# Tiles of the block products, and the planned spacing of the S5 input blocks

## Chip, core and metric

The kernel runs on one core of a Trainium2 chip. The metric is the device time of one execution in microseconds (us), and the figure quoted is the median over runs. The engines are TensorE (PE, with its weight loads as PEld), VectorE (DVE), ScalarE (ACT) and GpSimd (POOL); SyncE (SP) issues nearly all DMAs.

## What is computed

One layer of an encoder block on a sequence of 1024 positions with 1024 features, float32:

```python
xn = rmsnorm(h)
u, z_a, v, b_g, c_g, z_b, g_a, g_b = split(xn @ w_in)        # w_in is 1024 x 8192
y = D*u + S5_forward(u) + S5_backward(u)                      # 64 groups of 16 features, 64 states
y = gelu(y); y = y * sigmoid(y @ w_glu); y_a = y * silu(z_a)
y_b = b_g * (conv3(c_g * v) + conv_b) * silu(z_b)
merged = sigmoid(g_a) * (y_a @ w_branch_a) + sigmoid(g_b) * (y_b @ w_branch_b)
out = rmsnorm(h + merged @ w_out)
```

## The kernel before, in words

Each float32 matrix is split into a high and a low part, and a product is three products of parts (high x high, high x low, low x high), each over eight blocks of 128. One matmul here is 128 x 128 by 128 x 512.

The work goes by stages. First the input is normalised and turned, and the tables of the S5 branch are built. Then come the **projections**: 36 items of 48 matmuls each, one for every 128 columns of most of `w_in`. An item loads 512 KB of weights (`wr_p`), and most items store 512 KB of results to DRAM. Beside the items runs the **S5 branch**, in 16 blocks of four groups. An input block (`input_block`, line 534) loads two tables of 512 KB, `bdt_x` and `pwt_x`, and 256 KB of `u`; DVE joins the tables (lines 554 to 557), PE multiplies (`xps`, line 566) and ACT puts the result into the states. After four input blocks DVE runs the scan; then for each block come the output map, the correction `ks` (lines 578 and 580, behind the matmuls `kf` and `kb`) and the output products `yps` (line 594). `bdt_x` and `pwt_x` have two buffers each, so a `bdt` load waits for PE's use of the block before the last, and a `pwt` load for DVE's work on it.

The order of PE's and DVE's instructions is the order in which the code issues them. It is set by estimates: `est["pe"]` and `est["dve"]` count planned microseconds, and `at["t"]` (line 574) says when the next input block is due. Work of an engine that is not so fixed (ACT, SP) is placed by the scheduler.

Behind the projections the rest of `w_in` is done as **block products** (`gates`, `seven`). A pair of column blocks takes seven products of 12 matmuls (a Strassen form) instead of eight: in order `B11`, `T2`, `T1`, `T3`, `B21`, `B22`, `T4`. Each goes to a PSUM tile; DVE adds it into the results (`plus`). There are 12 pairs in `pairs7`. Some products read combined inputs `sx0` to `sx3` that DVE and ACT build beforehand (`combinations`, lines 833 to 841 and 806, 807): `sx2` and `sx3` only once all S5 work is out. The weights of a pair are combined one pair ahead by `prep`; those of the first pair are made during the last item. While a pair runs, DVE also does the convolution and the gating of earlier pairs (`jobs`); so pairs are fuller or lighter for DVE, by turns of three.

PSUM holds eight banks of 512 columns: four single tiles (`bank`, turned round in order) and two wide tiles of two banks each (`mm_tile`). In a pair, `T1` and `T3` are the two halves of one wide tile and `T4` is half of the other; the other four products are in single banks.

After the pairs come four products of the whole size: with `w_branch_b` (its input `yb` is read back from DRAM), with `w_glu`, with `w_branch_a`, and with `w_out`, and then the last normalisation.

Of the kernel before, what the change touches and what calls it, by code (L numbers as in the profile page):

```python
# [45 lines left out]
def bcast(ap, axis, n):  # L46
    shape = list(ap.shape)
    shape.insert(axis, n)
    return ap.unsqueeze(axis).to_broadcast(shape)
# [3 lines left out]
def block_kernel(  # L53
# [32 lines left out]
    def bank(name):  # L86
        return bgp.tile([P, 512], F32, tag="bg", name=name)

    def mm_tile(name):
        return mmp.tile([P, D], F32, tag="mm", name=name)  # L90
# [80 lines left out]
    with ExitStack() as st:  # L171
# [150 lines left out]
        f = math.factorial  # L322
# [176 lines left out]
    est = {"pe": 0.0, "dve": 6.0}  # L499
    parts = []  # L500

    def vec(us):
        est["dve"] = max(est["dve"], est["pe"]) + us

    def part(ready, us, fn):
        p_ = {"ready": ready, "us": us, "fn": fn, "end": None}
        parts.append(p_)
        return p_
# [11 lines left out]
    def ssm(sp, other):  # L520
# [3 lines left out]
        def load_u(blk, name):  # L524
            U = sp.tile([P, 4, P], F32, tag="U", name=f"U_{name}", bufs=3)
            base = ud[blk // 2][:, :]
            nc.sync.dma_start(out=U, in_=bass.AP(tensor=base.tensor, offset=base.offset + 4 * (blk % 2) * H * D,
                                                 ap=[[P, P], [H * D, 4], [1, P]]))
            return U

        SBs, lasts = {}, {}
        at = {"n": 0, "t": 20.0}

        def input_block():
            n = at["n"]
            q = n // 4
            if n % 4 == 0:
                SBs[q] = turn_p.tile([P, P, 2, GQ], F32, tag=f"Y{q % 2}", name=f"SB{q}")
            SB = SBs[q]
            nm = f"x{n}"  # L540
            U = load_u(n, nm)
            rep = []
            for src, outer, tag in ((bd, [[NG * 2 * P, H], [0, T]], "X0"), (pw, [[0, H], [NG * 2 * P, T]], "X2")):
                r_ = turn_p.tile([P, 4, 2, P], F32, tag=f"X{int(tag[1]) + n % 2}", name=f"{'bdt' if src is bd else 'pwt'}_{nm}")
                base = src[:, :]
                nc.sync.dma_start(
                    out=r_, in_=bass.AP(tensor=base.tensor, offset=base.offset + 4 * n * 2 * P,
                                        ap=outer + [[1, 4 * 2 * P]]))
                rep.append(r_)

            g_ = sp.tile([P, 4, 2, P], F32, tag="dv", name=f"g_{nm}", bufs=1)
            Wi, pw_ = rep
            er, ei = (bcast(pw_[:, :, ri], 2, 2) for ri in range(2))
            V.tensor_tensor(out=g_, in0=Wi, in1=er, op=ALU.mult)
            V.tensor_tensor(out=pw_, in0=Wi[:, :, ::-1], in1=ei, op=ALU.mult)
            V.tensor_tensor(out=Wi[:, :, 0], in0=g_[:, :, 0], in1=pw_[:, :, 0], op=ALU.subtract)
            V.tensor_tensor(out=Wi[:, :, 1], in0=g_[:, :, 1], in1=pw_[:, :, 1], op=ALU.add)
            vec(3.8)
            gl = 4 * (n % 4)

            def into():
                for ri in range(2):
                    xps = bank(f"xps{ri}_{nm}")
                    x3 = xps.rearrange("p (j c) -> p j c", j=4)
                    for j in range(4):
                        nc.tensor.matmul(out=xps[:, P * j:P * j + P], lhsT=Wi[:, j, ri, :],  # L566
                                         rhs=U[:, j, :], start=True, stop=True)
                    dst = SB[:, :, ri, gl:gl + 4].rearrange("p k g -> p g k")
                    S.copy(out=dst[0:NG], in_=x3[0:NG])  # L569
                    S.copy(out=dst[NG:P, :, ::-1], in_=x3[NG:P])  # L570

            lasts[q] = part(est["dve"] + 0.5, 1.8, into)
            at["n"] += 1
            at["t"] = max(at["t"], est["pe"] - 6.0) + 8.0

        def lags(b):
            ks, kf, kb = b["ks"], b["kf"], b["kb"]
# [239 lines left out]
    HK = K // 2  # L817
    half = (slice(0, 512), slice(512, D))
# [94 lines left out]
    def seven(p, w):  # L913

        sx = late["S"]
        u, i = pairs7[p]
        A = lambda o, h: [(xnh[o + k][:, half[h]], xnl[o + k][:, half[h]]) for k in range(HK)]
        o_ = [held(q, f"v{i + q}") if u == 2 else t4(f"go{p}_{q}") for q in range(2)]
        at = lambda q, h: o_[q][:, half[h]]
        wide = {}  # L920

        def prod(n, xs, place=None):
            if place is None:
                ps = bank(f"g{n}_{p}")
            else:
                if place[0] not in wide:
                    wide[place[0]] = mm_tile(f"gw{place[0]}_{p}")
                ps = wide[place[0]][:, half[place[1]]]
            for k in range(HK):
                for i_, (l, r) in enumerate(((0, 0), (0, 1), (1, 0))):  # L930
                    nc.tensor.matmul(out=ps, lhsT=w[n][l][:, k, :], rhs=xs[k][r],  # L931
                                     start=k == 0 and i_ == 0, stop=k == HK - 1 and i_ == 2)
            est["pe"] += 12 * 0.2266
            return ps

        def plus(q, h, ps, in_, end=False):
            V.tensor_tensor(out=at(q, h), in0=ps, in1=in_, op=ALU.add)  # L937
            vec(0.66)
            if end and u >= 6:
                S.activation(out=at(q, h), in_=at(q, h), func=AF.Sigmoid)  # L940

        g = prod("B11", A(0, 0))
        yield 0
        S.copy(out=at(0, 0), in_=g)
        g = prod("T2", sx["2"])
        yield 1
        plus(0, 1, g, at(0, 0))
        g = prod("T1", sx["1"], (0, 0))
        yield 2
        plus(1, 0, g, at(0, 1))  # L950
        g = prod("T3", sx["3"], (0, 1))
        yield 3
        plus(1, 1, g, at(1, 0), True)
        plus(0, 1, g, at(0, 1))
        g = prod("B21", A(HK, 0))
        yield 4
        plus(0, 0, g, at(0, 0), True)
        g = prod("B22", sx["4"])
        yield 5
        plus(1, 0, g, at(1, 0), True)  # L960
        g = prod("T4", A(HK, 1), (1, 0))
        yield 6
        plus(0, 1, g, at(0, 1), True)
        if u >= 6:
            for q in range(2):
                nc.sync.dma_start(out=(gbd if u == 7 else gad)[i + q], in_=o_[q])
        elif u == 2:
            vs[:] = o_
        elif u == 4:
            later_c(i, o_, vs)  # L970
        elif u == 3:
            later_b(i, o_)
# [115 lines left out]
    for i in range(K):  # L1088
        ps = product(w_branch_b[0][:, P * i:P * i + P], ybh, ybl, f"ob{i}")
# [25 lines left out]
    for i in range(K):  # L1115
        ps = product(w_glu[0][:, P * i:P * i + P], ygh, ygl, f"glu{i}", ks=ks)
# [21 lines left out]
    for i in range(K):  # L1138
        ps = product(w_branch_a[0][:, P * i:P * i + P], yah, yal, f"oa{i}")
# [30 lines left out]
    for h in range(2):  # L1170
        for t in range(T):
# [3 lines left out]
            for c, (o, n) in enumerate(cuts):  # L1175
                ps = bank(f"o{h}_{t}_{c}")
# [57 lines left out]
```

## Time and profile before

| | |
|---|---|
| Time, three runs | 1186.35 us median (1179.81 to 1187.08) |
| The profiled execution | 1184.2 us, span 1182.4 us |
| PE busy | 1132.7 us, 96% of the span |
| DVE busy | 818.7 us, 69% |
| ACT busy | 462.4 us, 39% |
| DMA | 167.79 MB, 138 GB/s of HBM over the span |

Matmuls overlap, so PE's busy time says only that it seldom stands still; how fast it goes is read from the starts of successive rows in its timeline. A wait is shown in square brackets behind the row that it delays, with what ended it.

### The profile page before, as it was taken

The numbers are of one execution on the slowest core, as the hardware profiler recorded it, in microseconds if no ns is written. First come the engines' busy times: TensorE is split into PE (matmuls) and PEld (weight loads), VectorE is DVE, ScalarE is ACT, GpSimd is POOL, SyncE is SP. The second block draws the span as 40 slices with busy tenths as digits, with TensorE's granted clock in tenths as the row PEclk, the third lists the DMA queues.
The fourth block names the chain that finished last, engine by engine and source line by source line (L and its number), as shares of the span: only waits on it lengthen the run. The fifth ranks groups of instructions, "written<-read, shape, count | busy, mean of one in ns | idle before, by whom it ended". The sixth has DMA issues, their size and how long they took to land.

```text
span 1182.4 us, 15042 instructions
## 1 busy us (share of the span) xinstructions
PE 1132.7 (96%) x5782; PEld 935.1 (79%) x5782; DVE 818.7 (69%) x1303; ACT 462.4 (39%) x556; POOL 14.4 (1%) x59
## 2 busy tenths in 40 slices
PE   6999989999999999999899999999999999999997
PEld 4777868888888888888677777777788888887886
DVE  6856579768877997877786868777378347446234
ACT  6343761664276255174332222223255225123111
POOL 2000000000000000000000000000000000000000
PEclk9999999999999999999899999999999999999999
DMA  8339983377347335433423141416757434227002
GB/s 265 95 134 259 253 232 116 125 207 190 116 132 195 116 104 152 124 99 107 143 60 118 43 135 36 142 36 230 268 184 252 169 107 139 93 89 261 6 36 106
DMA packets 166459, 167.79 MB, mean 142 GB/s; under 512 B 11852, under 2 KB 138996, under 8 KB 166260
## 3 DMA queue, kind: packets, MB, share of 16 engines
q1 hardware_dynamic: 166244, 166.65, 46.0%
q8 instruction: 45, 0.74, 0.2%
q14 instruction: 26, 0.21, 0.1%
q10 hardware_dynamic: 144, 0.20, 0.0%
HBM read 119.63 MB, written 42.99 MB: 138 GB/s over the span
## 4 chain that ended last, share of the span: by engine, by line
PE 85%; DVE 6%; DMA 4%; issue 2%; ACT 2%; SPq 0%; POOL 0%; POOLq 0%; DVEq 0%; ACTq 0%
PE ps_p L136 30%; PE gB L931 8%; PE ps_glu L136 7%; PE gw L931 7%; PE o L1181 7%; PE ps_oa L136 7%; PE ps_ob L136 7%; PE gT L931 3%; PE ps_u L136 2%; PE xps_x L566 2%; DMA bdt_x<-bd 2%; PE yps_y L596 1%; PE yps_y L595 1%; PE yps_y L594 1%; DVE fT L886 1%
## 5 line engine op out<-in xcount | busy, mean ns | idle before, releaser
L136 PE MATMUL ps_p<-xnh,wh_p 128*128 128x512 f32 x576 | 182.1, 398 | 0.0
L136 PE MATMUL ps_p<-xnl,wh_p 128*128 128x512 f32 x576 | 178.1, 390 | 0.0
L136 PE MATMUL ps_p<-xnh,wl_p 128*128 128x512 f32 x576 | 177.8, 390 | 0.0
L136 PEld LDWEIGHTS ps_p<-xnl,wh_p 128*128 128x128 f32 x576 | 108.5, 188 | 23.1
L136 PEld LDWEIGHTS ps_p<-xnh,wl_p 128*128 128x128 f32 x576 | 108.4, 188 | 23.0
L136 PEld LDWEIGHTS ps_p<-xnh,wh_p 128*128 128x128 f32 x576 | 105.9, 189 | 22.9 <-issue 3.2
L686 DVE TENSOR_TENSOR SB<-SB,st 128x32 f32<-128x32 f32 (+2 forms) x232 | 98.7, 425 | 8.0
L682 DVE TENSOR_TENSOR st<-SB,ac 128x64 f32<-128x64 f32 (+2 forms) x116 | 80.1, 690 | 7.0 <-DMA ac<-acd 3.9
L119 ACT CAST wh_p<-wr_p 128x1024 fp32r<-128x1024 f32 x36 | 37.9, 1052 | 119.2 <-PE ps_p L136 80.6
L1181 PE MATMUL o<-wo,mh 128*128 128x512 f32 (+1 forms) x272 | 79.7, 377 | 1.3 <-ACT mh L806 1.3
L806 ACT CAST hT<-fT 128x512 fp32r<-128x512 f32 x48 | 28.8, 619 | 126.0 <-DVE fT L886 51.5
L931 PE MATMUL gw<-sx,hT 128*128 128x512 f32 x192 | 61.9, 405 | 14.0 <-DVE go L937 10.2
L1181 PEld LDWEIGHTS o<-wo,mh 128*128 128x128 f32 x272 | 50.0, 188 | 11.0 <-ACT mh L806 1.7
L931 PEld LDWEIGHTS gw<-sx,hT 128*128 128x128 f32 x192 | 36.2, 194 | 26.1 <-ACT hT L806 16.3
L120 DVE TENSOR_TENSOR wl_p<-wr_p,wh_p 128x1024 fp32r<-128x1024 f32 x36 | 43.9, 1220 | 15.0 <-ACT wh_p L119 15.0
L1181 PE MATMUL o<-wo,ml 128*128 128x512 f32 (+1 forms) x136 | 51.3, 377 | 0.3 <-DVE ml L807 0.3
L569 ACT COPY SB<-xps_x 64x512 f32<-64x512 f32 x32 | 35.3, 1104 | 30.4 <-PE xps_x L566 30.1
L614 ACT COPY Sx_y<-SB 64x1016 f32<-64x1016 f32 x16 | 33.5, 2094 | 17.8 <-DVE SB L686 17.5
L136 PE MATMUL ps_oa<-yal,wh_oa 128*128 128x512 f32 x128 | 39.5, 390 | 0.0
L136 PE MATMUL ps_oa<-yah,wl_oa 128*128 128x512 f32 x128 | 39.4, 389 | 0.0
L136 PE MATMUL ps_glu<-ygh,wh_glu 128*128 128x512 f32 x128 | 39.4, 389 | 0.0
L136 PE MATMUL ps_glu<-ygh,wl_glu 128*128 128x512 f32 x128 | 39.4, 389 | 0.0
(292 smaller groups left out, 2271.0 us busy)
## 6 DMA issues: line engine op xcount, KB each, us to landing
wr_p<-in_w_in_dram SPq DMA_DIRECT2D x36, 512.0 KB
bdt_x<-bd SPq DMA_DIRECT2D x16, 512.0 KB
pwt_x<-pw SPq DMA_DIRECT2D x16, 512.0 KB
wr_a<-in_w_in_dram SPq DMA_DIRECT2D x12, 512.0 KB
wr_b<-in_w_in_dram SPq DMA_DIRECT2D x12, 512.0 KB
x<-in_x_dram SPq DMA_DIRECT2D x8, 512.0 KB
ud<-us SPq DMA_DIRECT2D x8, 512.0 KB
U_x<-ud SPq DMA_DIRECT2D x16, 256.0 KB
```

The lines of the kernel that those rows point to most:

```text
L119: S.copy(out=hi, in_=raw)
L120: V.tensor_tensor(out=lo, in0=raw, in1=hi.bitcast(F32), op=ALU.subtract)
L136: nc.tensor.matmul(out=ps[:, 512 * h:512 * h + 512], lhsT=l[:, k, :], rhs=r[k][h] if isinstance(r[k], tuple) else r[k][:, 512 * h:512 * h ...
L566: nc.tensor.matmul(out=xps[:, P * j:P * j + P], lhsT=Wi[:, j, ri, :], rhs=U[:, j, :], start=True, stop=True)
L569: S.copy(out=dst[0:NG], in_=x3[0:NG])
L594: nc.tensor.matmul(out=o, lhsT=b["Wl"][:, j, 0, :], rhs=b["Sx"][:, j, 0, :], start=True, stop=False)
L614: S.copy(out=Sx[0:NG, :, :, 1:P], in_=zsrc[0:NG, :, :, 0:P - 1])
L682: V.tensor_tensor(out=t_[:, 0:n].rearrange("p b r s g -> p b r (s g)"), in0=bcast(z.rearrange("p b r g -> p b (r g)"), 2, 2), in1=bcast(ac ...
L686: V.tensor_tensor(out=o, in0=o, in1=t_[:, 0:n, :, s_], op=ALU.add)
L806: S.copy(out=hi, in_=src)
L931: nc.tensor.matmul(out=ps, lhsT=w[n][l][:, k, :], rhs=xs[k][r], start=k == 0 and i_ == 0, stop=k == HK - 1 and i_ == 2)
L1181: nc.tensor.matmul(out=ps[:, 0:n], lhsT=l[:, ts_], rhs=r, start=(k == 0 and i == 0), stop=(k == K - 1 and i == 2))
```

## The change

There are two edits. In `seven` every product now has a PSUM tile of its own: `T1` and `T4` each take the first half of a wide tile, and `T3` goes to a single bank. So a pair uses five single banks in turn out of four, and both wide tiles, each half used. And in `input_block` the next block's due time moves by 9.0 planned microseconds instead of 8.0.

```diff
--- before.py
+++ after.py
@@ -571,7 +571,7 @@
 
             lasts[q] = part(est["dve"] + 0.5, 1.8, into)
             at["n"] += 1
-            at["t"] = max(at["t"], est["pe"] - 6.0) + 8.0
+            at["t"] = max(at["t"], est["pe"] - 6.0) + 9.0
 
         def lags(b):
             ks, kf, kb = b["ks"], b["kf"], b["kb"]
@@ -917,15 +917,9 @@
         A = lambda o, h: [(xnh[o + k][:, half[h]], xnl[o + k][:, half[h]]) for k in range(HK)]
         o_ = [held(q, f"v{i + q}") if u == 2 else t4(f"go{p}_{q}") for q in range(2)]
         at = lambda q, h: o_[q][:, half[h]]
-        wide = {}
-
-        def prod(n, xs, place=None):
-            if place is None:
-                ps = bank(f"g{n}_{p}")
-            else:
-                if place[0] not in wide:
-                    wide[place[0]] = mm_tile(f"gw{place[0]}_{p}")
-                ps = wide[place[0]][:, half[place[1]]]
+
+        def prod(n, xs, wide=False):
+            ps = mm_tile(f"gw{n}_{p}")[:, half[0]] if wide else bank(f"g{n}_{p}")
             for k in range(HK):
                 for i_, (l, r) in enumerate(((0, 0), (0, 1), (1, 0))):
                     nc.tensor.matmul(out=ps, lhsT=w[n][l][:, k, :], rhs=xs[k][r],
@@ -945,10 +939,10 @@
         g = prod("T2", sx["2"])
         yield 1
         plus(0, 1, g, at(0, 0))
-        g = prod("T1", sx["1"], (0, 0))
+        g = prod("T1", sx["1"], True)
         yield 2
         plus(1, 0, g, at(0, 1))
-        g = prod("T3", sx["3"], (0, 1))
+        g = prod("T3", sx["3"])
         yield 3
         plus(1, 1, g, at(1, 0), True)
         plus(0, 1, g, at(0, 1))
@@ -958,7 +952,7 @@
         g = prod("B22", sx["4"])
         yield 5
         plus(1, 0, g, at(1, 0), True)
-        g = prod("T4", A(HK, 1), (1, 0))
+        g = prod("T4", A(HK, 1), True)
         yield 6
         plus(0, 1, g, at(0, 1), True)
         if u >= 6:
```

The second edit moves instructions on every engine from the first S5 block on. Three places are shown.

On PE, the eighth input block (`xps0_x7`, `xps1_x7`) among the matmuls of the projections; `ps_p6` is item 6, `xnh0` to `xnh7` and `xnl0` to `xnl7` the blocks of its input. A row with x2 is two matmuls. Before:

```order
L136 MATMUL ps_p6_1622<-xnh0_161,wh_p6_1549 128x512 x2
L136 MATMUL ps_p6_1622<-xnl0_169,wh_p6_1549 128x512 x2
L136 MATMUL ps_p6_1622<-xnh0_161,wl_p6_1550 128x512 x2
L566 MATMUL xps0_x7_1632<-U_x7_1589,bdt_x7_1591 128x128 x4
L566 MATMUL xps1_x7_1639<-U_x7_1589,bdt_x7_1591 128x128 x4
L136 MATMUL ps_p6_1622<-xnh1_162,wh_p6_1549 128x512 x2
L136 MATMUL ps_p6_1622<-xnl1_170,wh_p6_1549 128x512 x2
L136 MATMUL ps_p6_1622<-xnh1_162,wl_p6_1550 128x512 x2
```

Now:

```order
L136 MATMUL ps_p6_1593<-xnh7_168,wh_p6_1520 128x512 x2
L136 MATMUL ps_p6_1593<-xnl7_176,wh_p6_1520 128x512 x2
L136 MATMUL ps_p6_1593<-xnh7_168,wl_p6_1521 128x512 x2
L566 MATMUL xps0_x7_1684<-U_x7_1645,bdt_x7_1647 128x128 x4
L566 MATMUL xps1_x7_1691<-U_x7_1645,bdt_x7_1647 128x128 x4
L136 MATMUL ps_p7_1702<-xnh0_161,wh_p7_1629 128x512 x2
L136 MATMUL ps_p7_1702<-xnl0_169,wh_p7_1629 128x512 x2
L136 MATMUL ps_p7_1702<-xnh0_161,wl_p7_1630 128x512 x2
```

It moved from behind the first three of the 24 rows of item 6 to behind the last: 21 rows. The sixth block moved by six rows, and so did the fourth.

On DVE, the last correction (`ks_y15`), with the combined inputs (`s`, `sx`, `xf`) around it; `sz` and `wl_p` belong to the items. Before:

```order
L841 TENSOR_TENSOR s24_0_4759<-s31_0_4596,xf0_4566 128x512
L841 TENSOR_TENSOR s24_0_4759<-xf4_4588,s24_0_4759 128x512
L807 TENSOR_TENSOR sx0_3_4565<-s24_0_4759,sx0_2_4564 128x1024
L757 TENSOR_TENSOR sz_4771<-ps_p32_4601,sz_4771 128x1024
L120 TENSOR_TENSOR wl_p34_4805<-wr_p34_4802,wh_p34_4804 128x1024
L578 SCALAR_TENSOR_TENSOR ks_y15_4793<-mask_160,Dk_159,ks_y15_4793 128x16
L580 TENSOR_TENSOR ks_y15_4793<-kf_y15_4775,ks_y15_4793 128x16
L833 TENSOR_TENSOR xf1_4838<-xnh1_162,xnl1_170 128x1024
L833 TENSOR_TENSOR xf5_4846<-xnh5_166,xnl5_174 128x1024
L841 TENSOR_TENSOR s31_1_4854<-xf1_4838 128x512
```

Now:

```order
L841 TENSOR_TENSOR s24_0_4812<-s31_0_4648,xf0_4618 128x512
L841 TENSOR_TENSOR s24_0_4812<-xf4_4640,s24_0_4812 128x512
L807 TENSOR_TENSOR sx0_3_4617<-s24_0_4812,sx0_2_4616 128x1024
L833 TENSOR_TENSOR xf1_4845<-xnh1_162,xnl1_170 128x1024
L757 TENSOR_TENSOR sz_4854<-ps_p33_4659,sz_4854 128x1024
L120 TENSOR_TENSOR wl_p35_4867<-wr_p35_4864,wh_p35_4866 128x1024
L578 SCALAR_TENSOR_TENSOR ks_y15_4841<-mask_160,Dk_159,ks_y15_4841 128x16
L580 TENSOR_TENSOR ks_y15_4841<-kf_y15_4823,ks_y15_4841 128x16
L833 TENSOR_TENSOR xf5_4893<-xnh5_166,xnl5_174 128x1024
L841 TENSOR_TENSOR s31_1_4901<-xf1_4845 128x512
L841 TENSOR_TENSOR s31_1_4901<-xf1_4845,xf5_4893 128x512
```

The `sz` and `wl_p` ahead of the correction are now those of the next item (33 and 35 instead of 32 and 34), which stood behind it before, between `sx1` and `sx2`; one `xf1` moved ahead. On PE the last S5 product (`yps_y15`) stood 51 rows of projection matmuls before the end of the projections and stands 30 rows before it now.

On DVE, where the weights of the first pair (`fT1_0` to `lB22_0`) are prepared. Before:

```order
L807 TENSOR_TENSOR sx2_4935<-s31_2_4952,sx2_4935 128x1024
L841 TENSOR_TENSOR s24_2_4969<-s31_2_4952,xf2_4936 128x512
L841 TENSOR_TENSOR s24_2_4969<-xf6_4944,s24_2_4969 128x512
L807 TENSOR_TENSOR sx2_4935<-s24_2_4969,sx2_4935 128x1024
L833 TENSOR_TENSOR xf3_4991<-xnh3_164,xnl3_172 128x1024
L833 TENSOR_TENSOR xf7_5003<-xnh7_168,xnl7_176 128x1024
L886 TENSOR_TENSOR fT1_0_5011<-wr_b0_5001,wr_a0_4999 128x512
L886 TENSOR_TENSOR fT2_0_5013<-wr_b0_5001,fT1_0_5011 128x512
L807 TENSOR_TENSOR la_0_5022<-wr_a0_4999,ha_0_5021 128x1024
L807 TENSOR_TENSOR lT2_0_5026<-fT2_0_5013,hT2_0_5025 128x512
```

Now:

```order
L807 TENSOR_TENSOR sx2_4959<-s31_2_4980,sx2_4959 128x1024
L886 TENSOR_TENSOR fT1_0_5001<-wr_b0_4993,wr_a0_4991 128x512
L886 TENSOR_TENSOR fT2_0_5003<-wr_b0_4993,fT1_0_5001 128x512
L807 TENSOR_TENSOR la_0_5012<-wr_a0_4991,ha_0_5011 128x1024
L807 TENSOR_TENSOR lT2_0_5016<-fT2_0_5003,hT2_0_5015 128x512
L807 TENSOR_TENSOR lT1_0_5026<-fT1_0_5001,hT1_0_5025 128x512
L886 TENSOR_TENSOR fT3_0_5029<-wr_b0_4993 128x512
L807 TENSOR_TENSOR lT3_0_5038<-fT3_0_5029,hT3_0_5037 128x512
L886 TENSOR_TENSOR fT2_0_5003<-wr_a0_4991,fT2_0_5003 128x512
L807 TENSOR_TENSOR lB22_0_5049<-wr_b0_4993,hB22_0_5048 128x512
L841 TENSOR_TENSOR s24_2_5058<-s31_2_4980,xf2_4960 128x512
L841 TENSOR_TENSOR s24_2_5058<-xf6_4968,s24_2_5058 128x512
```

The second half of `sx2` and the two `xf` of `sx3` came before that preparation and now come after it; `sx3` follows in both.

On SP's queue the loads of the input blocks change places with those of the items: `bdt_x3`, of the fourth block, stood right behind that block's own `pwt_x3`; it now stands behind `pwt_x3`, the weights of item 5 and `pwt_x4`, the fifth block's.

## Rows read from the trace of the kernel before

**Rows 1.** Page: busy us (share) of two engines; the chain that ended last, by engine.

```profile
PE 1132.7 (96%) x5782; PEld 935.1 (79%) x5782; DVE 818.7 (69%) x1303; ACT 462.4 (39%) x556; POOL 14.4 (1%) x59
...
PE 85%; DVE 6%; DMA 4%; issue 2%; ACT 2%; SPq 0%; POOL 0%; POOLq 0%; DVEq 0%; ACTq 0%
```

**Rows 2.** Waits of PE: who waited for whom, total us, times, longest.

```profile
PE gw L931 <- DVE go L937: 10.2, 9, 1.5
...
PE xps_x L566 <- DVE bdt_x L556: 5.2, 2, 4.3
...
PE gw L931 <- DVE v L937: 3.9, 3, 1.3
...
PE gT L931 <- ACT sx L806: 2.5, 1, 2.5
```

**Rows 3.** Timeline of PE over one pair: start, us, line, xcount, [idle <- releaser].

```profile
597.38 0.39 PE L931 MATMUL gB<-xnh,ha 128*128 128x512 f32 x1
...
607.17 0.70 PE L931 MATMUL gw<-sx,hT 128*128 128x512 f32 x2 [1.47 <-DVE go L937]
...
610.01 0.39 PE L931 MATMUL gB<-xnh,ha 128*128 128x512 f32 x1
...
618.17 0.39 PE L931 MATMUL gB<-xnh,ha 128*128 128x512 f32 x1
```

**Rows 4.** Timeline of PE: first product of the last pair, first output product.

```profile
802.74 0.39 PE L931 MATMUL gB<-xnh,ha 128*128 128x512 f32 x1
...
822.91 0.62 PE L136 MATMUL ps_ob<-xnh,wh_ob 128*128 128x512 f32 x2
```

**Rows 5.** Timeline of DVE in the pair of rows 3.

```profile
606.35 0.68 DVE L937 TENSOR_TENSOR go<-gw,go 128x512 f32<-128x512 f32 x1
...
610.21 1.29 DVE L937 TENSOR_TENSOR go<-gw,go 128x512 f32<-128x512 f32 x2
...
620.84 1.30 DVE L1019 TENSOR_TENSOR go<-go,xnl 128x512 f32<-128x512 f32 x2
```

**Rows 6.** Windows: us, busy (x) PE PEld DVE ACT POOL, PEclk, DMA, GB/s.

```profile
612.00:633.00 21.00, 19.71 (x87) 16.04 (x87) 18.91 (x29) 4.65 (x7) 0.00 (x0) 1.00 0.41 131
...
633.00:654.00 21.00, 20.12 (x90) 16.37 (x89) 12.25 (x19) 4.98 (x8) 0.00 (x0) 1.00 0.24 70
...
654.00:675.00 21.00, 19.53 (x87) 15.86 (x86) 16.66 (x24) 7.15 (x10) 0.00 (x0) 1.00 0.18 51
```

**Rows 7.** Timeline of PE: the sixth and the eighth S5 input block.

```profile
152.43 2.05 PE L566 MATMUL xps_x<-U_x,bdt_x 128*128 128x128 f32 x16 [0.89 <-DVE bdt_x L556]
...
171.73 3.28 PE L566 MATMUL xps_x<-U_x,bdt_x 128*128 128x128 f32 x16 [4.33 <-DVE bdt_x L556]
```

**Rows 8.** Window over the first eight S5 input blocks, columns as in rows 6.

```profile
95.00:166.00 71.00, 68.14 (x405) 56.95 (x406) 46.49 (x56) 43.51 (x45) 0.00 (x0) 0.98 0.93 242
```

**Rows 9.** Timeline of SP's queue: two loads of S5 input blocks.

```profile
118.93 0.52 SPq L546 DMA_DIRECT2D bdt_x<-bd  x1
...
125.81 0.51 SPq L546 DMA_DIRECT2D pwt_x<-pw  x1
```

**Rows 10.** Timeline of PE: first block products after the projections.

```profile
570.71 0.39 PE L931 MATMUL gB<-xnh,ha 128*128 128x512 f32 x1
...
578.15 0.57 PE L931 MATMUL gT<-sx,hT 128*128 128x512 f32 x1 [2.52 <-ACT sx L806]
...
580.43 1.05 PE L931 MATMUL gw<-sx,hT 128*128 128x512 f32 x2
```

**Rows 11.** Timeline of DVE: from the last ks to the end of sx3.

```profile
540.21 0.17 DVE L580 TENSOR_TENSOR ks_y<-kf_y,ks_y 128x16 f32<-128x16 f32 x1
...
550.99 1.22 DVE L757 TENSOR_TENSOR sz<-ps_p,sz 128x1024 f32<-128x1024 f32 x1 [1.13 <-ACT sz L756]
...
578.13 1.23 DVE L807 TENSOR_TENSOR sx<-s,sx 128x1024 fp32r<-128x1024 f32 x1 [1.11 <-ACT sx L806]
```

**Rows 12.** Window behind the stall of rows 10, columns as in rows 6.

```profile
577.00:586.00 9.00, 6.75 (x15) 4.64 (x15) 4.21 (x7) 2.28 (x3) 0.00 (x0) 0.62 0.32 106
```


## Prediction

> **What bounds the kernel now.** I read the page first, then the waits of TensorE (PE), then the three places where PE waits: timelines of PE and of VectorE (DVE) there, and tables by window. PE is busy for 96% of the span and carries 85% of the chain that ended last; DVE is busy for 69% [rows 1]. So an edit is worth what it does to PE's gaps, and DVE counts where PE waits for it. The gaps that matter are three [rows 2]. In the block products twelve waits, 14.1 us together, are for a DVE sum. Early in the projections two waits, 5.2 us, are for an S5 input block. At the first block product 2.5 us are for the last combined input `sx3`.
>
> The reader is to see in [rows 3] what one of the twelve costs. A pair runs from the first `B11` matmul, 597.38, to the next, 618.17: 20.79 us. From 610.01 to 618.17 the products `B21`, `B22` and `T4`, 36 matmuls, go through without a gap: 8.16 us, 0.2267 us each. A pair has 84 matmuls, so it would take 19.04 us; 1.75 us are lost, all at `T3`: it waits 1.47 us, its first matmuls cannot overlap the last of `T1`, and it starts more slowly.
>
> **Edit 1, the tiles.** `T3` waits because it writes the other half of the wide tile from which DVE still reads `T1`: it goes on right behind that sum, which runs from 606.35 for 0.68 us [rows 3, 5]. With a bank of its own it has no such reader. Over ten pairs PE takes 802.74 - 597.38 = 205.36 us, 14.96 us more than ten times 19.04; the last pair takes 20.17 us, 1.13 more [rows 3, 4]; for the first pair I take 0.9, as it has the same wait. Together 17.0 us. No instruction is added.
>
> What could take the place of that wait? Five products now share four banks. `B22` takes the bank of its own pair's `B11`; `B11`, `T2`, `T3` and `B21` take those of the previous pair's `T2`, `T3`, `B21` and `B22`. The tightest is `T2` behind the two sums of the previous `T3`. In the pair shown these begin at 610.21 and last 1.29 us [rows 5], done by 611.5; the next `T2` would start at 618.17 - 1.75 + 12 x 0.2267 = 619.1. That is 7.6 us of slack.
>
> DVE is the cover to watch, since each pair gets 1.1 to 1.75 us shorter. In three successive windows of 21 us it is busy 18.9, 12.3 and 16.7 us, 47.8 in all [rows 6]; three pairs would take PE 57.1 us, so DVE keeps up over three. In the full one it falls behind PE by about the 1.75 us that PE gains, works on without a pause to the end of the row at 620.84 [rows 5], and catches up in the light one. A lag of under 2 us is inside the 7.6 us of slack. It would cost only at the end: the chain from the last sums and the loads of `yb` to the first output products is DVE's, and the full pair `pairs7[10]` and the last stand just ahead of it. Their gain is 1.7 + 1.1 = 2.8 us; between 0 and 2.8 of it may be given back there, and I take 1.0.
>
> The granted clock reads 1.00, the 2.4 GHz level, in the windows that hold these waits [rows 6], and after the wait `T3` takes 2.84 us, to 610.01, against 12 x 0.2267 = 2.72 [rows 3]. So I add nothing for the clock. The Trainium skill, "TensorE: Matmul & The Clock Gate", section "A second HAM failure mode: psum-queue depth-cycling", has short idle times between matmul groups, as banks are cycled, throw the array back to its lower clock. By that rule the twelve waits would hold a loss in clock too, and the change would bring more; the trace disagrees, with 1.00.
>
> **Edit 2, the spacing.** It changes no work, but the order on every engine. The eighth S5 block stands 21 rows of projection matmuls later in PE's order; a row is two matmuls, 0.453 us, so PE comes to it 9.5 us later. Now it waits 4.33 us for it and then takes 3.28 us instead of 2.05, at a lowered clock; the sixth block waits 0.89 us [rows 7]. What is late there is the load: the DMA queues are 0.93 busy and move 242 GB/s through this stretch [rows 8]. Moving the block by 7/8 of an item lets 7/8 of 1 MB (half weights, half results) go ahead of it: 0.9 MB at 242 GB/s, 3.7 us. So the block comes 3.7 us later and PE 9.5 us later: 5.8 us more room, over 4.33. The sixth block is six rows later, 2.7 us, against 1.1 us of loads: 1.6 us, over 0.89. So both waits should go: 4.33 + 1.23 + 0.89 = 6.4 us. Against it stands SP's queue: the fourth block's `bdt`, issued at 118.93, now stands behind the fifth block's `pwt`, which must wait until DVE is done with the third block and was issued at 125.81 [rows 9]: some 7 us later. PE comes to the fourth block only six rows, 2.7 us, later. If the queue decides, a new wait of up to 4 us takes part of the gain. Bounds: a gain from 2 to 6.4; I take 6.4, as the DMA, not the order of issue, is what the full queues show.
>
> Now the other end. The last S5 part stands 30 rows before the end of the projections instead of 51: 21 rows, again 9.5 us nearer. What follows it on DVE in one chain is the building of `sx1` to `sx3` and the preparation of the first pair. Before, the last correction `ks` starts at 540.21 and `sx3` is complete at 578.13 + 1.23 = 579.4 [rows 11]; the projections end at 570.71 [rows 10], so `sx3` comes 8.7 us after. PE's next use of it stands 2.72 + 2.04 us after that end, at 575.5, and it loses 4.3 us up to `T1`, which starts at 580.43 instead of 576.15 [rows 10]. In the new order the chain starts 9.5 us later against the end; a `sz` and a `wl_p` no longer stand in it, a wait of 1.13 us, 1.23 us, and a piece of DVE work of about that size: I take 3.4 us, as they overlap a little [rows 11]. An `xf` moves ahead of the correction, which delays it as much as it shortens the rest: nothing. So `sx3` comes 9.5 - 3.4 = 6.1 us later against PE, and PE, which waits for nothing else there, loses 6.1 us more. Bounds: 3 us, if the correction, held up now by scalar copies, comes earlier; 9.5, if nothing is taken out.
>
> After that stall the clock is granted at 0.62 on average [rows 12], so most of it is at 1.2 GHz. After the longer stall I expect the same and add nothing, with 0 to 2 us as bounds.
>
> **The sum.** -17.0 + 1.0 - 6.4 + 6.1 = -16.3 us. The profiled execution took 1184.2 us (its span 1182.4 and 1.8 around it); 1184.2 - 16.3 = 1167.9. That execution is 2.2 us under the median of the runs, 1186.35, which lie between 1179.81 and 1187.08. I keep 1168. About 1%, 12 us, is what a measurement of this kernel can tell from no change.
>
> **Rivals.**
> 1. DVE becomes the bound of the full pairs. For it: 18.9 us busy beside 19.04. Against it: 7.6 us of slack and a light pair behind each. If each of the four full pairs gave its 1.75 us back, 7 us: 1175.
> 2. The S5 tail costs more: no row taken out of the chain, 9.5 us, and a slow clock for 2 us more. For it: all of `sx2` and `sx3` is one chain. Then 5.4 us on top: 1173.
> 3. The early waits stay, or move to the fourth block. For it: DMA is full and the queue's order is worse there. Then 4.4 to 6.4 us are missing: 1173.
> 4. `T3` waits on after all: the wait is for another DVE step than the sum of `T1`, such as a weight. Against it: it ends 0.14 us after that sum, in the row. Then edit 1 gives nothing: 1184.
> 5. Slower: the S5 work falls behind for good. All sixteen blocks are planned a microsecond wider; if DVE, which is 69% busy on average and fuller here, passed that on in each of the four groups instead of using its pauses, the last correction would fall behind the end of the projections. PE then stands still for that chain. It decides from the point where the correction comes 16 us later than I place it; then the gain is gone, and at 30 us it is 1198. Against it: the order has the last part 30 rows, 13.6 us, before the end.
> 6. The waits between products cost clock, and free it. Each `T3` would run at half pace now, 2.72 us lost twelve times, 33 us: 1135. Against it: granted clock 1.00. The page named above is the source of this one.
>
> **Chances.** The forecast 0.57, rival 1 0.08, rival 2 0.12, rival 3 0.14, rival 4 0.04, rival 5 0.04, rival 6 0.01. The forecast's own bounds: gates -17 to -14, early -6.4 to -2, tail +3 to +9.5, and 3 us for the spread of the runs. The range from 1160 to 1178 takes in rivals 1 to 3 and leaves out 4, 5 and 6 and the edges of the others. Faster by over 1% (under 1174.5) are the forecast and about six in ten of rivals 1 to 3: 0.78. Within 1%: the rest of these and rival 4: 0.18. Slower: rival 5, 0.04.
>
> **What would show it.** No wait of a block product for a DVE sum, and pairs 19.0 us apart from `B11` to `B11`; if some are 20.8, rival 1 or 4. No wait at the sixth and eighth `xps`, granted clock near 1 from 166 to 176 us; a wait at the fourth block shows rival 3. `T2` of the first pair waiting about 9 us for `sx3`; above 13, rival 2. And a wait for `yb` at the first output product of about 2 us. I would be wrong if the pairs shorten and the time does not, since nothing behind them but that one wait is seen to take it back.

## The result, and the profile after

The changed kernel takes 1169.43 us (1167.2 to 1169.96, four runs), the kernel before 1186.71 us; the ratio is 0.9863, 95% interval 0.9823 to 0.9903. That is 17 us less by the medians, where 18 were forecast (1168). The two profiled executions are 14.5 us apart (spans of 1182.4 and 1167.9 us), and the places below are compared by these.

The page after, its busy time and shares:

```profile
PE 1131.8 (97%) x5782; PEld 936.6 (80%) x5782; DVE 817.0 (70%) x1303; ACT 462.1 (40%) x556; POOL 14.5 (1%) x59
```

The waits of PE after: who waited for whom, us in total, times, longest.

```profile
PE gT L925 <- ACT sx L806: 7.5, 1, 7.5
PE yps_y L596 <- DMA toe_y<-ks_y: 1.8, 1, 1.8
...
PE xps_x L566 <- DVE bdt_x L556: 1.2, 2, 0.7
PE xps_x L566 <- DMA U_x<-ud: 1.2, 1, 1.2
...
PE ps_ob L136 <- DVE ybl L807: 1.1, 2, 0.5
```

Against [rows 2], the twelve waits of products for DVE are gone, the waits at the S5 input blocks fell from 5.2 to 1.2 us, and the one for `sx3` rose from 2.5 to 7.5. The wait for `toe_y` is new (the products are at line 925 now, their sums at 931).

The timeline of PE over the same pair as in [rows 3]: start, us, line, matmul, count.

```profile
598.48 0.39 PE L925 MATMUL gB<-xnh,ha 128*128 128x512 f32 x1
...
606.64 0.62 PE L925 MATMUL gT<-sx,hT 128*128 128x512 f32 x2
...
609.36 0.39 PE L925 MATMUL gB<-xnh,ha 128*128 128x512 f32 x1
...
617.52 0.39 PE L925 MATMUL gB<-xnh,ha 128*128 128x512 f32 x1
```

And DVE there, the sum of `T1` first:

```profile
607.45 0.68 DVE L931 TENSOR_TENSOR go<-gwT,go 128x512 f32<-128x512 f32 x1
```

The pair takes 617.52 - 598.48 = 19.04 us instead of 20.79. `T3` starts at 606.64, three products of 2.72 us behind the pair's start, while DVE comes to the sum of `T1` only at 607.45: `T3` no longer waits for that sum. Two windows show DVE (third busy time) in a full pair and in the light one behind it, columns as in [rows 6]:

```profile
617.52:636.56 19.04, 19.04 (x86) 15.77 (x84) 17.71 (x27) 4.52 (x7) 0.00 (x0) 1.00 0.55 171
636.56:655.60 19.04, 19.04 (x86) 15.77 (x84) 11.52 (x17) 4.55 (x7) 0.00 (x0) 1.00 0.26 76
```

The S5 input blocks on PE, fourth, seventh and eighth:

```profile
138.87 2.05 PE L566 MATMUL xps_x<-U_x,bdt_x 128*128 128x128 f32 x16 [0.69 <-DVE bdt_x L556]
...
166.85 2.05 PE L566 MATMUL xps_x<-U_x,bdt_x 128*128 128x128 f32 x16 [0.54 <-DVE bdt_x L556]
178.31 1.95 PE L566 MATMUL xps_x<-U_x,bdt_x 128*128 128x128 f32 x16
```

The eighth block waits for nothing and takes 1.95 us, where [rows 7] had 4.33 and 3.28. Small new waits stand at the fourth and the seventh (the expectations below call the seventh the eighth).

The first block products on PE, and the chain ahead of them on DVE (the last `ks`, the end of `sx3`):

```profile
568.08 0.39 PE L925 MATMUL gB<-xnh,ha 128*128 128x512 f32 x1
...
580.71 0.79 PE L925 MATMUL gT<-sx,hT 128*128 128x512 f32 x1 [7.48 <-ACT sx L806]
```

```profile
547.46 0.17 DVE L580 TENSOR_TENSOR ks_y<-kf_y,ks_y 128x16 f32<-128x16 f32 x1
...
580.69 1.22 DVE L807 TENSOR_TENSOR sx<-s,sx 128x1024 fp32r<-128x1024 f32 x1 [1.11 <-ACT sx L806]
```

`sx3` is complete at 581.91, 13.83 us behind the end of the projections (568.08); by [rows 10, 11] it was 8.65.

The starts on PE divide each execution into stages. All numbers are differences of two starts in the timeline, in us.

| stage | before | after | difference | forecast |
|---|---|---|---|---|
| start to the first S5 input block | 109.72 | 110.85 | +1.13 | 0 |
| from there to the first block product | 460.99 | 457.23 | -3.76 | -6.4 |
| first pair | 26.67 | 30.40 | +3.73 | +5.2 (+6.1 and -0.9) |
| eleven pairs behind it | 225.53 | 209.44 | -16.09 | -16.1 |
| product with `w_branch_b` | 88.12 | 89.19 | +1.07 | +1.0 |
| the rest | 271.37 | 270.79 | -0.58 | 0 |
| sum (the spans) | 1182.4 | 1167.9 | -14.5 | -16.3 |

### The profile page after: what moved, and what is told of

It is laid out like the page before. It is cut to its first block, busy times and chain, and to the rows that moved or that the text cites. A ratio compares the mean times of both kernels' runs of the same rounds, so it can differ in the third digit from the quotient of the medians.

```text
span 1167.9 us, 15029 instructions
## 1 busy us (share of the span) xinstructions
PE 1131.8 (97%) x5782; PEld 936.6 (80%) x5782; DVE 817.0 (70%) x1303; ACT 462.1 (40%) x556; POOL 14.5 (1%) x59
## 4 chain that ended last, share of the span: by engine, by line
PE 82%; DMA 7%; DVE 6%; ACT 2%; issue 2%; SPq 1%; POOL 0%; POOLq 0%; ACTq 0%; DVEq 0%
PE ps_p L136 27%; PE ps_glu L136 7%; PE o L1175 7%; PE ps_oa L136 7%; PE ps_ob L136 7%; PE gB L925 7%; PE gwT L925 5%; PE gT L925 5%; PE ps_u L136 3%; DMA bdt_x<-bd 2%; PE xps_x L566 2%; PE yps_y L596 1%; PE yps_y L595 1%; PE yps_y L594 1%; DMA ybt<-ybd 1%
## 5 line engine op out<-in xcount | busy, mean ns | idle before, releaser
L925 PE MATMUL gT<-sx,hT 128*128 128x512 f32 x192 | 60.3, 394 | 7.9 <-ACT sx L806 7.5
L925 PEld LDWEIGHTS gT<-sx,hT 128*128 128x128 f32 x192 | 36.2, 189 | 16.7 <-ACT sx L806 7.9
L136 PE MATMUL ps_oa<-yah,wh_oa 128*128 128x512 f32 x128 | 39.4, 389 | 0.0
```

The lines of the kernel that those rows point to most:

```text
L136: nc.tensor.matmul(out=ps[:, 512 * h:512 * h + 512], lhsT=l[:, k, :], rhs=r[k][h] if isinstance(r[k], tuple) else r[k][:, 512 * h:512 * h ...
```

## The experiments

The ratios are to the kernel before, run on the same chip in between. The stages are named as in the table above; they come from one profiled execution each, so a difference of a microsecond or two between two of them can be spread.

### The changed kernel again, and each edit alone

`after_again` is the changed kernel, unchanged. `tiles_only` has edit 1 and the spacing of before, `spacing_only` edit 2 and the tiles of before. Against the changed kernel, `tiles_only` is:

```diff
-            at["t"] = max(at["t"], est["pe"] - 6.0) + 9.0
+            at["t"] = max(at["t"], est["pe"] - 6.0) + 8.0
```

Expected of `after_again`:

> The changed kernel once more, as the measure for the others of this call. Every theory: 17 us under the kernel before, a ratio of 0.986; pairs 19.04 us apart; 0.5 to 1 us of wait at the fourth and at the eighth S5 input block; 7 to 8 us of wait of T2 in the first pair for sx3.

Expected of `tiles_only`:

> Edit 1 alone: the new tiles, spacing 8.0. My theory: all of the gain is the tiles'. Pairs 19.04 us apart, no product waits for DVE, 16.1 us less over the last eleven pairs and about 1 in the first, 1 us given back at the first output product: a ratio of 0.986 to 0.987, the same as the changed kernel within 2 us. The early waits of 0.9 and 4.3 us stay, and T2 of the first pair waits 2.5 us as before. Rival 1 (the spacing is worth 3 us by itself): ratio 0.989. Rival 2 (the spacing costs 3 us by itself, its stall before the first pair being more than it saves): ratio 0.984.

Expected of `spacing_only`:

> Edit 2 alone: spacing 9.0, old tiles. My theory: the early waits shrink by about 4 us and the stall of the first pair grows by about 5, so the two cancel: a ratio of 0.999 to 1.003. T3 waits 0.9 to 1.5 us in each of the twelve pairs, which stay 20.2 to 20.8 us apart. Rival 1: 0.997. Rival 2: 1.003 or more.

| kernel | us | ratio (95%) | S5 block to products | first pair | eleven pairs |
|---|---|---|---|---|---|
| after again | 1168.47 | 0.9842 (0.9817 to 0.9866) | 456.84 | 30.70 | 209.44 |
| tiles only | 1171.53 | 0.9864 (0.9839 to 0.9889) | 462.74 | 24.50 | 209.44 |
| spacing only | 1185.20 | 0.9990 (0.9974 to 1.0006) | 458.01 | 31.12 | 225.61 |

The waits of PE in `spacing_only`:

```profile
PE gw L931 <- DVE go L937: 10.2, 9, 1.5
...
PE gT L931 <- ACT sx L806: 7.5, 1, 7.5
PE gw L931 <- DVE v L937: 3.9, 3, 1.3
PE xps_x L566 <- DVE bdt_x L556: 2.2, 2, 1.7
```

The products wait 14.1 us for DVE here, as in [rows 2], and the stall for `sx3` is that of the changed kernel. The gain is the tiles'; the spacing gives about 3 us in its first place, takes about 4.5 in its second, and its time is that of before within its interval. On top of the new tiles it gives 5.5 to 5.9 us in the first place and takes 5.9 to 6.2 in the second. What sign their sum has there is not settled: the intervals of `after_again` and `tiles_only` overlap.

### Is it the load or the queue that makes the eighth block late?

`eight_and_half` has the new tiles and a spacing of 8.5: the eighth block is later, the end of the S5 work is where it was.

> New tiles with a spacing of 8.5: the eighth S5 input block stands 9 rows of matmuls later than before instead of 21, and the last S5 product stands where it stood before, 51 rows ahead of the end of the projections. My theory, that the early waits and the stall of the first pair are two separate prices: the eighth block's wait falls from 4.3 to about 2 us (4.1 us more on PE, 1.6 us more loads ahead), T2 of the first pair waits 2.5 us as before, so 2 to 3 us under tiles_only, a ratio of 0.984. Rival (what is taken from the early waits comes back anywhere later, since the S5 loads are the bound of that stretch): the same as tiles_only, 0.9865.

It took 1167.02 us, ratio 0.9828 (0.9803 to 0.9852), which would fit, though the interval overlaps that of `tiles_only`. The profiled execution does not fit; at 1172.46 us it is the longest of six, and the others took 1166.12 to 1167.34, so what happened at these blocks in them is not shown. In the profile the eighth block waits no more, but the sixth does, for longer, and goes at half pace behind it (the granted clock from 158 to 163 us is 0.50):

```profile
158.46 3.75 PE L566 MATMUL xps_x<-U_x,bdt_x 128*128 128x128 f32 x16 [5.69 <-DVE bdt_x L556]
```

From the first S5 block to the products this execution takes 462.92 us, no less than that of `tiles_only`. SP's queue tells why; in the same kernel, starts and durations of two of its loads:

```profile
144.94 0.52 SPq L546 DMA_DIRECT2D pwt_x<-pw  x1
...
146.19 0.52 SPq L546 DMA_DIRECT2D bdt_x<-bd  x1
```

The second is the sixth block's `bdt`. PE was done with its buffer when the fourth block ended, at 136.68 + 2.02 = 138.7. But ahead of it in the queue stands the `pwt` of the seventh block, and this waits for DVE's work on the fifth. So the load goes out 7.5 us late.

The same is to be seen in the kernel before. SP's queue there, ahead of the eighth block's `bdt` (162.04):

```profile
153.62 0.54 SPq L765 DMA_DIRECT2D gbd<-sg  x1
161.57 0.37 SPq L116 DMA_DIRECT2D wr_p<-in_w_in_dram  x1
162.04 0.54 SPq L546 DMA_DIRECT2D bdt_x<-bd  x1
```

DVE in that stretch and at the eighth block's tables, and what the DMA engines did from the time when the buffer was free, and in the last 4 us (columns as in [rows 6]):

```profile
160.33 1.22 DVE L120 TENSOR_TENSOR wl_p<-wr_p,wh_p 128x1024 fp32r<-128x1024 f32 x1
...
168.35 1.23 DVE L554 TENSOR_TENSOR g_x<-bdt_x,pwt_x 128x1024 f32<-128x1024 f32 x1 [4.21 <-DMA bdt_x<-bd]
```

```profile
154.54:162.04 7.50, 7.50 (x42) 6.25 (x41) 6.50 (x8) 4.51 (x5) 0.00 (x0) 1.00 0.48 145
...
158.00:162.00 4.00, 4.00 (x26) 3.40 (x25) 3.90 (x5) 1.05 (x2) 0.00 (x0) 1.00 0.07 29
```

PE left the buffer at 152.43 + 2.05 = 154.5 [rows 7]. SP stood still from 154.2 to 161.57 for a buffer of projection weights, which DVE let go with `wl_p`. DVE then waited 4.21 us for the late load, and PE for DVE. From 154.54 to 162.04 the DMA engines were 0.48 busy, in the last 4 us of that 0.07. They were nearly full over the whole stretch [rows 8], but not where the load was late.

What the spacing changed is seen in SP's queue of the changed kernel (the `bdt` of the seventh block, then of the eighth):

```profile
156.48 0.52 SPq L546 DMA_DIRECT2D pwt_x<-pw  x1
157.09 0.55 SPq L546 DMA_DIRECT2D bdt_x<-bd  x1
...
159.39 1.22 SPq L546 DMA_DIRECT2D bdt_x<-bd  x1
```

The eighth block's load now goes out 1.25 us after its buffer is free (the sixth block ends at 156.19 + 1.95 = 158.14). The seventh's is late instead, by 6.2 us (the fifth ends at 148.95 + 1.95 = 150.90), but costs only the 0.54 us seen above. So the queue still holds loads back; the new order moved the delay to a block with more room.

The next kernel takes that load out of SP's queue: new tiles, spacing 8.0, and

```diff
-                nc.sync.dma_start(
+                (nc.gpsimd if src is bd else nc.sync).dma_start(
```

> New tiles, spacing 8.0 (as in tiles_only), with one edit: the loads of bdt_x are issued on GpSimd's queue instead of SP's, so that they stand behind no other load. My theory now: the early waits come from the order on SP's queue. Before, the eighth block's bdt is issued at 162.04, behind a weight load wr_p issued at 161.57, though PE was done with its buffer at 154.5. So here that load is issued some 7 us earlier against the start of the block before, the waits of 0.9 and 4.3 us at the sixth and eighth block go, and the stall of the first pair stays at 2.5 us: 5 to 6 us under tiles_only, ratio 0.981 to 0.982. Rival (the theory of my prediction: the DMA queues are full and decide): the data come no earlier whoever issues them, the waits stay, ratio 0.986.

It took 1165.46 us, ratio 0.9834 (0.9808 to 0.9861). None of the eight early `xps` waits, which speaks for the queue; the time alone would not, as the interval overlaps that of `tiles_only`. And a new wait came ahead of them:

```profile
101.58 0.39 PE L649 MATMUL kf_y<-W_y,Bt 64*32 64x128 f32 x1 [6.38 <-DVE W_y L636]
```

On GpSimd the first two `bdt` loads, 1 MB, are issued at 82.4:

```profile
82.39 1.18 POOL L546 DMA_DIRECT2D bdt_x<-bd  x2 [56.10 <-ACT wh_p L119]
```

In `tiles_only` they go out at 96.7 and 98.6, behind the `ce_y` that DVE needs for `W_y`; `ce_y` is issued at 92.15 there and at 96.76 here. `pool_from_third` therefore leaves them on SP:

```diff
-                (nc.gpsimd if src is bd else nc.sync).dma_start(
+                (nc.gpsimd if src is bd and n > 1 else nc.sync).dma_start(
```

> As bdt_pool (new tiles, spacing 8.0), but the first two bdt loads stay on SP and only the third to the sixteenth are issued on GpSimd. In bdt_pool the early waits were gone, but a new wait of 6.4 us stood ahead of the first S5 block, at kf. My theory: that one comes from the first two bdt loads alone, which went out ahead of loads that were needed sooner; without it the early waits are gone and nothing else changes: 5 to 6 us under tiles_only in its own span (1167.9), 1162 to 1163 us, ratio 0.978 to 0.980. Rival: with bdt on a queue of its own other loads come later whichever are moved, and some 5 us show up at another place: ratio 0.983.

It took 1162.12 us, ratio 0.9796 (0.9767 to 0.9826). Its interval lies below that of `tiles_only`. From the first S5 block to the products it takes 455.85 us, 6.9 less than `tiles_only` (`pool_and_first_pair` below, with the same order there, takes 458.10). The `bdt` load into the sixth block's buffer, for the eighth, and then the sixth, seventh and eighth block on PE:

```profile
155.21 0.51 POOL L546 DMA_DIRECT2D bdt_x<-bd  x1 [9.45 <-PE xps_x L566]
```

```profile
152.97 1.95 PE L566 MATMUL xps_x<-U_x,bdt_x 128*128 128x128 f32 x16
160.21 1.95 PE L566 MATMUL xps_x<-U_x,bdt_x 128*128 128x128 f32 x16
167.45 1.95 PE L566 MATMUL xps_x<-U_x,bdt_x 128*128 128x128 f32 x16
```

The load goes out 0.3 us after the matmuls (152.97 + 1.95 = 154.92), and the eighth block waits for nothing, at the spacing of before. Taking `bdt` out of SP's queue also lets the loads behind it go earlier; what share of the gain is theirs is not shown.

At the third block there is now a wait of 1.54 us (2.37 in `pool_and_first_pair`), where the kernel before had none. DVE stands there for the `pwt` load, which SP issued at 112.38, and the DMA engines are full in that stretch:

```profile
123.72 1.23 DVE L554 TENSOR_TENSOR g_x<-bdt_x,pwt_x 128x1024 f32<-128x1024 f32 x1 [5.98 <-DMA pwt_x<-pw]
```

```profile
111.00:126.00 15.00, 14.51 (x75) 12.04 (x73) 6.28 (x7) 10.25 (x10) 1.19 (x2) 1.00 0.98 243
```

So here a load that is issued in time comes late, with the DMA engines 0.98 busy: at the third block they are the likely cause, which no run tests, and not at the eighth.

The Trainium skill, "Trainium Kernel Development and Optimization", section "Key Constraints", says that issuing DMAs from several engines saves only issue time, as all run on the same DMA engines. Here the measurement differs: what was saved is the wait of one load behind another's semaphore.

### What the spacing costs at the other end

`pool_from_third_nine` is the same kernel with the spacing of 9.0.

> The same with the spacing of the change, 9.0. The early waits are gone in both, so the two differ by what the spacing costs at the other end alone. My theory: T2 of the first pair waits 7.5 instead of 2.5 us for sx3, and a wait for toe of 1.5 us comes back: 5 to 6 us slower than pool_from_third, ratio 0.983. Rival (the stall comes with the S5 loads and not with the spacing): the same as pool_from_third within 2 us.

It took 1167.87 us, ratio 0.9837 (0.9810 to 0.9865): 5.8 us more by the medians, and the five runs of each (1160.95 to 1162.79, and 1165.37 to 1168.44) do not overlap. The first pair takes 29.73 us against 24.55, and PE waits 7.5 us for `sx3` against 2.5. The projections take 455.42 us against 455.85. So without the queue's wait the spacing saves nothing and costs its stall, 5.2 us.

`first_pair` is the changed kernel with one product moved, in the first pair only:

```diff
+        if p == 0:
+            b21 = prod("B21", A(HK, 0))
         g = prod("T2", sx["2"])
...
-        g = prod("B21", A(HK, 0))
+        g = prod("B21", A(HK, 0)) if p else b21
```

> The changed kernel with one edit: in the first pair B21, which does not read sx0 to sx3, goes ahead of T2; its sum stays where it was. My theory, that PE waits there for the DVE chain to sx3 and for nothing else: the wait of T2 falls from 7.5 us by the 2.72 us of B21 to 4.8, the rest is unchanged: 2.7 us under the changed kernel, ratio 0.982. Rival (the wait is PE's own, from the slow clock or the bank of B11): the wait stays at 7.5 and the time at 0.984 to 0.986.

1165.98 us, ratio 0.9837 (0.9817 to 0.9857). The wait falls to

```profile
577.67 0.80 PE L925 MATMUL gT<-sx,hT 128*128 128x512 f32 x1 [4.98 <-ACT sx L806]
```

and the first pair to 26.71 us from 30.40 and 30.70 in the two profiles of the changed kernel. The wait is for the chain on DVE and ACT, as the theory has it; it fell by 2.5 us, about the length of the product (2.72). The pair gained 1.2 to 1.5 us more than that. `T1`, behind the stall, took 3.64 us here and 4.59 and 4.92 in the other two. But with the same stall of 7.48 us it took 3.73 to 3.94 in the profiles of `dve4`, `dve10` and `pool_from_third_nine`, and their first pairs 29.54 to 29.73 us. So most of that extra is spread of the clock from profile to profile, not the edit's. The time itself, between the 0.982 of the theory and the 0.984 to 0.986 of the rival, decides nothing.

Both together, spacing 8.0:

> pool_from_third and the edit of first_pair together, spacing 8.0: the version that should beat both kernels. T2 of the first pair waited 2.5 us for sx3; B21 ahead of it takes 2.72 us, so that wait goes but for the last half microsecond: 2.5 to 3 us under pool_from_third, 1159 to 1160 us, ratio 0.976. If the slow clock behind that wait goes with it, 2 us more.

`pool_and_first_pair` took 1159.86 us, ratio 0.9773 (0.9746 to 0.9801). It beats both kernels clearly, and `pool_from_third` by 2.3 us only in the medians, as their intervals overlap. Its first pair takes 20.50 us instead of 24.55. Two windows of 9 us behind the wait, of `pool_from_third` and of this kernel:

```profile
573.00:582.00 9.00, 8.23 (x29) 6.35 (x30) 6.09 (x9) 1.24 (x2) 0.00 (x0) 0.81 0.19 60
```

```profile
577.00:586.00 9.00, 8.23 (x37) 6.71 (x37) 7.73 (x11) 1.14 (x2) 0.00 (x0) 1.00 0.20 61
```

The wait that went is one of 2.55 us, the first pair gained 4.05. The other 1.5 us lie in the clock: behind 2.5 us of stall it is granted at 0.81 on average and `T1` takes 4.33 us, behind the 0.8 us that is left here at 1.00, which is 2.4 GHz, and `T1` takes 2.74.

### How far the tiles and their cover reach

`t4_with_t1` puts `T4` into the second half of `T1`'s wide tile and `T3` into the other one (against the changed kernel, with the wide tiles kept by number as before):

```diff
-        g = prod("T1", sx["1"], True)
+        g = prod("T1", sx["1"], (0, 0))
...
-        g = prod("T3", sx["3"])
+        g = prod("T3", sx["3"], (1, 0))
...
-        g = prod("T4", A(HK, 1), True)
+        g = prod("T4", A(HK, 1), (0, 1))
```

> The changed kernel, but T4 takes the second half of T1's wide tile and T3 a half of the other one, so T3 has a different tile than T1 but T1 and T4 share one. My theory: what matters is only that the next product does not write the tile that DVE still reads; T4 comes three products after T1, whose sum is long done: pairs 19.04 us apart, no product waits, the time of the changed kernel within 2 us. Rival (any shared wide tile costs a wait): T4 waits in each pair, pairs of 20 us and more, 1180 us.

One run: 1169.52 us. No product waits, all eleven pairs are 19.04 us. So a tile need not be a product's own; it must not be one that DVE still has to read.

`dve10` and `dve4` put sums that nobody reads on DVE, ten and four in each of ten pairs:

```diff
+                if 0 < p < len(pairs7) - 1 and n in (0, 2, 4, 6):
+                    V.tensor_tensor(out=spare, in0=..., in1=..., op=ALU.add)
```

Expected of `dve10`:

> The changed kernel with more work on DVE: ten spare sums of 128x512, 0.61 us each from start to start, in each of ten pairs (6.1 us a pair); nothing reads their result. It prices the cover of edit 1. In the changed kernel DVE is busy for 46.05 us in three successive pairs of 57.12. With 18.3 us on top it needs 64.4 us. If DVE's total is what sets the pairs from there (my theory), pairs settle at 21.4 us on average, and less the 7.6 us of slack that banks give once the time is some 15 to 24 us above the changed kernel, with products waiting for DVE. Rival (each product waits for its own sum, so that any work added ahead of a sum is paid in full): 61 us above it.

Expected of `dve4`:

> As dve10 with four spare sums in each of ten pairs, 2.44 us a pair, 24.4 us of DVE work in all. DVE then needs 53.4 us in three pairs of 57.12, so by the theory that its total sets the pairs nothing is lost: pairs 19.04 us apart, the changed kernel's time within 2 us. By the theory that the full pairs decide (17.7 + 2.44 = 20.1 us against 19.04), 1.1 us is lost in each of three or four full pairs, 3 to 5 us in all.

`dve4` took 1168.95 us, and its pairs are 19.04 us apart, with DVE 52.47 us busy in three of them (57.12 us). `dve10` took 1194.56 us, 25 us more than the changed kernel. The theory had 15 to 24, the rival 61. The eleven pairs, up to the first output product, take 230.6 us instead of 209.4. So the time lies just outside the theory's range. The products wait for DVE, as it had it, but what costs most is not a tile: it is the next pair's weights, and behind the pairs the input of the first output product:

```profile
PE gB L925 <- DVE la L807: 8.0, 2, 4.0
...
PE ps_ob L136 <- ACT xnh L806: 6.5, 2, 3.9
```

The first waits in time are smaller: `T2`, which the prediction had named as the tightest, waits 0.68 us at 637.81 and 1.03 us at 677.22.

## Why the prediction was right, point by point

**The tiles.** The term of -16.1 for the eleven pairs came out at -16.09, and the pairs at the 19.04 us that 84 matmuls take. In the first pair they gave 2.2 us (24.50 in `tiles_only` against 26.67) and not 0.9: the wait of `T3` there was 0.78 us, and much of the rest is the clock behind the stall for `sx3`, as `T1` took 4.34 us instead of some 5.2. Neither the lag of DVE in the full pairs nor the five products in four banks cost anything; `dve4` shows in one run that 2.4 us more per pair would have been hidden too. Rival 1 and rival 4 are out.

**The clock in the products** (rival 6). It read 1.00 before [rows 6] and reads 1.00 in the windows after; a pair gained its wait and the slower start of `T3` behind it (1.75 us in the pair of [rows 3]) and nothing more. The Trainium skill, "TensorE: Matmul & The Clock Gate", "A second HAM failure mode: psum-queue depth-cycling", has short idle times between matmul groups, frequent enough, throw the clock back. One wait of 0.9 to 1.5 us in each pair of about 20 us did not.

**The end of the pairs.** The forecast of +1.0 met +1.07, with 1.1 us of waits for `ybl` in place of the 2 expected. That the two agree is luck: the same stage takes 88.05 us in `after_again`, the same kernel, 90.24 in `eight_and_half` and 88.12 before.

**The early waits: the step that failed.** I set the loads that move ahead against 242 GB/s and concluded that "the DMA, not the order of issue, is what the full queues show". For the sixth and the eighth block the runs show the reverse. The waits were made by the order on SP's queue; a kernel with the old spacing and `bdt` on another queue loses them. That they went in the changed kernel too, with a granted clock of 1.00 from 166 to 176 us as forecast, is partly luck: its order happens to leave the delay at the seventh block. The size, -6.4, read -3.76 in this profile, and -5.5 and -5.9 against `tiles_only` (457.23 and 456.84 against 462.74). Profiles of the same order in `t4_with_t1` and `dve4` have 455.09 and 456.24, so it is known to a few microseconds only. The bound that I gave for the queue's order, a wait at the fourth block, came true, with 0.69 us. And a wait that I had not foreseen stands in the same stage: 1.8 us for `toe_y`, seen in the other kernels that keep the order of 9.0 too (1.4 to 1.8 us) and in none of the order of 8.0. The one of 1.18 us for `U_x` only moved.

**The stall for `sx3`.** The mechanism held: the last `ks` came 20.6 us ahead of the end of the projections instead of 30.5, 9.9 us nearer, for which I had 9.5. The chain from there to `sx3` became 4.7 us shorter (34.45 against 39.15), for which I had 3.4. So `sx3` came 5.2 us later against PE, not 6.1. The first pair paid 5.9 and 6.2 us for it in the two profiles of the changed kernel (against the 24.50 of `tiles_only`), 5.2 in `pool_from_third_nine`; the difference is again the clock behind the stall. That the first pair as a whole lost 3.73 us and not 5.2 comes from the tiles, which gave 2.2 there. The wait of 7.5 us is nearer the forecast of 9 than rival 2's 13.

**The sum.** Two terms were too large, by 2.6 us of gain and 1.5 us of loss, and partly cancel. Starting the first S5 block 1.1 us later is not the spacing: it starts between 109.51 and 111.23 in the kernels with the old spacing (leaving out `bdt_pool` with its wait ahead of it) and between 109.21 and 111.09 in those with the new one. Together the profiles end 1.8 us from the forecast, and the median 1.4.

## What to carry to other kernels

When a matmul waits for the engine that empties PSUM, look at which tile it writes: halves of one tile are one tile to the order of waits, and the next product should go to another. A late load is not yet a slow load: compare when it was issued with when its buffer came free, and read what stood ahead of it in its queue, before dividing bytes by bandwidth. And widening the spacing of early work is paid for where that work ends. Moving the blocked load to another queue costs nothing there, as long as it does not overtake a load that is needed sooner (6.38 us in `bdt_pool`).

## What the runs showed of the hardware

- SP's queue held a load back for 7.5 us behind another's wait, with the DMA engines 0.48 busy in that time and 0.07 in its last 4 us (the eighth block's `bdt` before). From GpSimd's queue the same load went out 0.3 us after its buffer was free (`pool_from_third`).
- After 7.48 us of stall most matmuls of `T1` ran at half pace in the changed kernel; the window from 580 to 590 us has a granted clock of 0.65. After the 0.8 us that `pool_and_first_pair` leaves, it was 1.00.
- What the clock costs behind a stall did not grow with its length here. `T1` takes 2.72 us at 2.4 GHz; it took 3.73 to 4.92 us behind 7.48 us of stall (five profiles), 3.64 behind 4.98, and 4.33 to 4.84 behind 2.5 to 2.7 us (four profiles of kernels with the new tiles).
- Profiles of kernels whose code is the same up to the first S5 block differ by over 1 us there (109.61 and 110.85 in `dve4` and the changed kernel), which is as much as several terms of a sum like this one. The changed kernel's second profile has 110.85 again, so whether the execution or the program makes the difference is open.
